# One VectorE sum of 1024 inputs in place of two of 512 for the later modulation vectors

## The chip, the core and the metric

The kernel runs on one core of one Trainium2 chip. The number that counts is the device time in microseconds (us) of one execution. The engines are TensorE (PE in the profile, its weight loads PEld), VectorE (DVE), ScalarE (ACT), GpSimd (POOL) and SyncE (SP). SP computes nothing; its queue issues nearly all DMA loads and stores here, strictly in the order in which they were written.

## The reference, cut to what matters

One layer of a diffusion backbone over 1024 latent tokens and 256 context tokens, all in float32, with a width of 1024:

```python
mod = einsum('bd,dn->bn', silu(c), w_ada) + b_ada       # 1024 inputs -> 6 * 1024
sh1, sc1, g1, sh2, sc2, g2 = split(mod, 6)
xn  = rmsnorm(h) * (1 + sc1) + sh1
mix = output projection of (differential attention over 1280 keys, gated 3-tap convolution)
h   = h + g1 * rmsnorm(mix)
xn  = rmsnorm(h) * (1 + sc2) + sh2
ff  = expert-choice mixture of 16 experts (router, gate, up, down)
h   = h + g2 * rmsnorm(ff)
```

The "later modulation vectors" are the last four of the six, `g1, sh2, sc2, g2`. They are needed only after attention.

## The kernel before, in words

The program has three stretches. The first (up to about 217 us in the profile) normalises the tokens, computes `sh1` and `sc1` on TensorE, and projects queries, keys and values. The second (217 to about 757 us) is attention, with the convolution and the output projection as filling work. The third holds the 16 experts.

**Attention.** 32 steps, one for each pair of a head (two score maps each) and a tile of 128 queries. The score maps `ps` (twice 128x1280) take 12 matmuls (L1090); VectorE finds the two row maxima `nm` (L1099), ScalarE takes the exponentials `e` (L1103), VectorE joins the two maps (L1117), TensorE transposes the result (`ptr`, L1130), ScalarE and VectorE split it into a high and a low part `ath`, `atl` (L1135, L1138), and on every second step 30 matmuls `po` multiply by the values. There is one buffer `ps` in PSUM: the scores of a step cannot start before both exponentials of the step before have read it. Scores run two steps ahead of the transposes. The code ahead of the loop (L1202 to L1212) makes the maps of the first two steps; these are "the first maps".

**Filling work.** Between these, `fill(n)` puts n matmuls of other work on TensorE, first those of the convolution's projection (`pf`, L675 to L679): 24 behind the first maps, 36 behind the second, then 36 in each step. Their weights come as blocks `wraw` (512 KB, L635), which ScalarE and VectorE split into `wh` and `wl`.

**The later modulation vectors.** `rows()` (L698 to L734) is a generator that computes them on VectorE. `w_ada` is laid out so that 128 outputs stand on the 128 partitions and the 1024 inputs along each; `silu(c)` lies in `silub`, repeated on all partitions. One instruction multiplies a tile `wa2` by `silub` and adds up along the row (L717, its sum read out by a second, short instruction). There are 4 vectors of 8 blocks, so 32 rows of 1024 inputs, 64 halves. A half is loaded (256 KB, L708) into one of three buffers; the next load into a buffer waits until the sum that read it is done. Four halves are asked for in each of the first steps (L1285), and two behind each of the first maps (L1210, L1211). When all 8 blocks of `g1` or `g2` are there, a small store writes the vector to DRAM element by element (`bS`, L732), so that it can be read back on all partitions.

**What sets the order.** SP's order, and TensorE's up to step 0, are the order of the program text. VectorE, ScalarE and, from step 0 on, TensorE are ordered by the framework's scheduler, from its own estimate of when operands are ready. In each engine's queue an instruction that waits holds up all behind it.

Of the kernel before, what the change touches and what calls it, by code (L numbers as in the profile page):

```python
# [10 lines left out]
F32 = mybir.dt.float32  # L11
# [4 lines left out]
OP = mybir.AluOpType  # L16
# [4 lines left out]
P = 128  # L21
D = 1024
# [5 lines left out]
KT = 8  # L28
# [124 lines left out]
def build(tc, nc, I, out, dbg=None):  # L153
    V, S, G, PE, SY = nc.vector, nc.scalar, nc.gpsimd, nc.tensor, nc.sync
# [3 lines left out]
    def f(ap):  # L158
        return ap.bitcast(F32)
# [11 lines left out]
    with es:  # L171
# [4 lines left out]
        sm = es.enter_context(tc.tile_pool(name="sm", bufs=4))  # L176
# [4 lines left out]
        def pool(stack, name, bufs=1, **kw):  # L181
            return stack.enter_context(tc.tile_pool(name=name, bufs=bufs, reuse_waits="tile", **kw))
# [329 lines left out]
        for i in range(10):  # L512
# [6 lines left out]
            for j in range(2):  # L519
                S.dma_start(out=vS[:, :, j, i, :].rearrange("h p e -> p h e"),  # L520
                            in_=f(hl[:, j, :]).rearrange("p (h e) -> p h e", h=H))
# [53 lines left out]
        rwp = pool(eR, "rwp", 3)  # L575
# [122 lines left out]
        def rows():  # L698
            sb = rwp.tile([P, D], F32, name="silub", bufs=1)
            SY.dma_start(out=sb, in_=bass.AP(tensor=sS.tensor, offset=sS.offset, ap=[[0, P], [1, D]]))  # L700
            src = deque((v, k, g) for v in (1, 2, 0, 3) for k in range(KT) for g in range(2))
            ws = deque()

            def load():
                if src:
                    v, k, g = src.popleft()
                    ws.append((v, k, g, rwp.tile([P, 512], F32, name="wa2")))
                    SY.dma_start(out=ws[-1][3], in_=I["wa2"][v, k, :, 512 * g:512 * g + 512])  # L708

            for _ in range(3):  # L710
                load()
            while ws:
                yield
                v, k, g, w = ws.popleft()
                if g:
                    part = sm.tile([P, 1], F32, name="part")
                V.scalar_tensor_tensor(w, w, 1.0, sb[:, 512 * g:512 * g + 512], op0=OP.mult, op1=OP.mult,  # L717
                                       accum_out=part if g else mv[:, v, k:k + 1])
                load()
                if g == 0:  # L720
                    continue
                V.tensor_add(mv[:, v, k:k + 1], mv[:, v, k:k + 1], part)
                if k == KT - 1:
                    V.tensor_add(mv[:, v, :], mv[:, v, :], late["bC"][:, v, :])
                    if v != 1:
                        V.scalar_tensor_tensor(mv[:, v, :], mv[:, v, :], 1.0 if v == 2 else 0.0,
                                               late["nC"][:, max(v - 1, 0), :], op0=OP.add, op1=OP.mult)
                    if v == 2:
                        lazy.append(fold)
                    elif v != 1:  # L730
                        def send(v=v):
                            SY.dma_start(out=bS[v // 3].rearrange("o (k p) -> p (o k)", p=P), in_=mv[:, v, :])  # L732

                        lazy.append(send)  # L734


        mv = cp.tile([P, 4, KT], F32, name="mv")
# [10 lines left out]
        def fold2():  # L748
            pw = bank([P, E], "pw")
            PE.matmul(pw, ones.to_broadcast([P, P]), cst2, start=True, stop=True)  # L750
            V.tensor_copy(out=cst2, in_=pw)

        rowgen = rows()
        woh, wol, worw = [None] * KT, [None] * KT, {}
        st = [dict() for _ in range(KT)]
# [328 lines left out]
        def scores(q, KK):  # L1084

            ps = psS.tile([P, 2, NK], F32, name="ps")
            for m in range(2):
                for (k0, n) in CH[m]:
                    for j in range(2):
                        PE.matmul(ps[:, m, k0:k0 + n], q[:, m, j, :], KK[:, m, k0:k0 + n], start=(j == 0),  # L1090
                                  stop=(j == 1))
            return ps, []

        def maxes(c):
            c[1].extend([ep.tile([P, NK], F32, name="e0", bufs=3), ep.tile([P, NK], F32, name="e1"),
                         sm.tile([P, 2], F32, name="l")])
            for m in range(2):
                c[1].append(sm.tile([P, 1], F32, name=f"nm{m}"))
                V.tensor_reduce(out=c[1][-1], in_=c[0][:, m, :], axis=AX.X, op=OP.max, negate=True)  # L1099

        def expo(c, m):
            e, l = c[1][m], c[1][2]
            S.activation(e, c[0][:, m, :], AF.Exp, bias=c[1][3 + m], accum_out=l[:, m:m + 1])  # L1103
# [98 lines left out]
        for i in range(2):  # L1202
            cs.append(scores(qq[i], KK[0]))
            maxes(cs[i])
            expo(cs[i], 0)
            expo(cs[i], 1)
            fill(F0)
            combine(cs[i], i)
            tick()
            next(rowgen)  # L1210
            next(rowgen)  # L1211
            fill(F1 * i)  # L1212
        steps = []

# [4 lines left out]
        for i, (h, qt) in enumerate(seq):  # L1219
# [62 lines left out]
                    hi(x2)  # L1282
                    lo(x2)
            if i < 16:
                for _ in range(4):  # L1285
                    next(rowgen, None)
            step()
            if odd:
# [207 lines left out]
        for e in range(E):  # L1496
            idx, g = cur[:2]
# [23 lines left out]
            for c in range(2):  # L1521
                w = chunk(e, 4 + c)
# [7 lines left out]
            if e + 1 < E:  # L1530
                y = x1.tile([P, D], F32, name="y")
                for dh in range(2):
                    S.activation(y[:, dh * 512:dh * 512 + 512], pys[dh], AF.Copy, scale=g[:, 0:1])
                G.indirect_dma_start(out=ffS[:, :], out_offset=bass.IndirectOffsetOnAxis(ap=idx[:, :1], axis=0),
                                     in_=y, in_offset=None, compute_op=OP.add)
# [37 lines left out]
        for i, grp in enumerate(TGR):  # L1573
            w = len(grp)
# [29 lines left out]
```

## Time and profile before

| | us |
|---|---|
| median of 3 runs | 1399.57 (1394.0 to 1402.64) |
| the profiled execution | 1401.37 |
| its span on the core | 1399.6 |
| TensorE busy in the span | 1259.0 (90%) |
| VectorE busy | 1104.3 (79%) |
| ScalarE busy | 805.7 (58%) |
| mean granted TensorE clock | 0.941 of full speed |

All rows are from one profiled execution. The span is the time from the first to the last instruction of the core; the 1.8 us on top of it lie outside the recorded instructions. Busy shares are averages over stretches with different limits, so the timelines, the waits and the windows of a stretch say more than the shares do.

### The profile page before, as it was taken

The numbers are of one execution on the slowest core, as the hardware profiler recorded it, in microseconds if no ns is written. First come the engines' busy times: TensorE is split into PE (matmuls) and PEld (weight loads), VectorE is DVE, ScalarE is ACT, GpSimd is POOL, SyncE is SP. The second block draws the span as 40 slices with busy tenths as digits, with TensorE's granted clock in tenths as the row PEclk, the third lists the DMA queues.
The fourth block names the chain that finished last, engine by engine and source line by source line (L and its number), as shares of the span: only waits on it lengthen the run. The fifth ranks groups of instructions, "written<-read, shape, count | busy, mean of one in ns | idle before, by whom it ended". The sixth has DMA issues, their size and how long they took to land.

```text
span 1399.6 us, 18794 instructions
## 1 busy us (share of the span) xinstructions
PE 1259.0 (90%) x6457; PEld 1028.7 (73%) x6457; DVE 1104.3 (79%) x2005; ACT 805.7 (58%) x1191; POOL 70.8 (5%) x56
## 2 busy tenths in 40 slices
PE   6999998999989699789762999999999999999990
PEld 3587886887878578677652888888888888877770
DVE  6963666988778667698686799999999998888885
ACT  6632112443434444453331888888888888888762
POOL 0000000000000000000001000000000001201012
PEclk8999999999999899999775999999999999999995
DMA  9359456554486963432287899999999999999736
GB/s 351 117 109 325 133 159 208 162 164 136 142 160 182 235 218 110 136 124 95 76 311 275 278 364 389 374 376 376 379 373 378 377 379 379 354 345 350 267 120 120
DMA packets 143376, 346.67 MB, mean 248 GB/s; under 512 B 17456, under 2 KB 59952, under 8 KB 142640
## 3 DMA queue, kind: packets, MB, share of 16 engines
q1 hardware_dynamic: 115520, 310.34, 63.4%
q0 software_dynamic: 5616, 20.45, 6.1%
q10 hardware_dynamic: 22144, 14.68, 3.7%
q8 instruction: 51, 0.84, 0.2%
q14 instruction: 45, 0.37, 0.1%
HBM read 296.65 MB, written 48.77 MB: 247 GB/s over the span
## 4 chain that ended last, share of the span: by engine, by line
PE 47%; DVE 8%; ACT 2%; issue 1%; DMA 1%; SPq 0%; POOL 0%; POOLq 0%; ACTq 0%; DVEq 0%
PE hg L167 4%; PE hg L168 4%; PE hg L166 4%; PE hu L166 4%; PE hu L167 4%; PE hu L168 4%; PE pyy L167 4%; PE pyy L168 4%; PE pyy L166 4%; PE ptt L1479 2%; PE pl L921 1%; DVE nm L1099 1%; PE ptt L1451 1%; PE pf L799 1%; PE ps L1090 1%
## 5 line engine op out<-in xcount | busy, mean ns | idle before, releaser
L163 DVE TENSOR_TENSOR wlo<-raw,whi 128x1024 fp32r<-128x1024 f32 x384 | 450.1, 1221 | 30.8 <-ACT whi L162 24.5
L162 ACT ACTIVATE whi<-raw 128x1024 fp32r<-128x1024 f32 x384 | 396.1, 1066 | 61.7 <-PE hu L168 24.9
L1103 ACT ACTIVATE e<-ps,nm 128x1280 f32<-128x1280 f32 x64 | 84.4, 1325 | 68.5 <-DVE nm L1099 61.3
L1099 DVE TENSOR_REDUCE nm<-ps 128x1 f32<-128x1280 f32 x64 | 92.8, 1485 | 16.0 <-PE ps L1090 15.9
L167 PE MATMUL pyy<-wlo,ach 128*128 128x512 f32 x256 | 101.3, 396 | 3.5 <-DVE wlo L163 3.1
L166 PE MATMUL hu<-whi,xsh 128*128 128x512 f32 x256 | 101.9, 398 | 0.0
L168 PE MATMUL hg<-whi,xsl 128*128 128x512 f32 x256 | 101.2, 395 | 0.8 <-DVE xsl L163 0.8
L167 PE MATMUL hg<-wlo,xsh 128*128 128x512 f32 x256 | 101.8, 398 | 0.0
L166 PE MATMUL hg<-whi,xsh 128*128 128x512 f32 x256 | 101.3, 396 | 0.0
L167 PE MATMUL hu<-wlo,xsh 128*128 128x512 f32 x256 | 100.8, 394 | 0.0
L168 PE MATMUL pyy<-whi,acl 128*128 128x512 f32 x256 | 100.2, 391 | 0.0
L168 PE MATMUL hu<-whi,xsl 128*128 128x512 f32 x256 | 99.9, 390 | 0.0
L1135 ACT ACTIVATE ath<-ptr 128x512 fp32r<-128x512 f32 (+1 forms) x96 | 47.5, 525 | 90.7 <-PE ptr L1130 90.4
L166 PE MATMUL pyy<-whi,ach 128*128 128x512 f32 x256 | 98.9, 402 | 0.0
L1090 PE MATMUL ps<-KK,q 128*128 128x512 f32 (+1 forms) x384 | 91.0, 384 | 7.8 <-ACT e L1103 6.2
L1090 PEld LDWEIGHTS ps<-KK,q 128*128 128x128 f32 x384 | 65.1, 202 | 18.8 <-ACT e L1103 7.4
L679 PE MATMUL pf<-xh,wl 128*128 128x512 f32 x192 | 77.7, 405 | 0.0
L677 PE MATMUL pf<-xl,wh 128*128 128x512 f32 x192 | 77.3, 403 | 0.0
L675 PE MATMUL pf<-xh,wh 128*128 128x512 f32 x192 | 77.0, 401 | 0.0
L1138 DVE TENSOR_TENSOR atl<-ptr,ath 128x512 fp32r<-128x512 f32 (+1 forms) x96 | 55.6, 596 | 13.8 <-ACT ath L1135 13.6
L167 PEld LDWEIGHTS pyy<-wlo,ach 128*128 128x128 f32 x256 | 48.2, 188 | 18.0 <-DVE wlo L163 8.2
L167 PEld LDWEIGHTS hg<-wlo,xsh 128*128 128x128 f32 x256 | 48.9, 191 | 11.5 <-DVE wlo L163 1.1
(293 smaller groups left out, 2728.8 us busy)
## 6 DMA issues: line engine op xcount, KB each, us to landing
raw<-in_we SPq DMA_DIRECT2D x384, 512.0 KB, 9.5
wa<-in_wa SPq DMA_DIRECT2D x64, 256.0 KB, 4.8
wraw<-in_wF SPq DMA_DIRECT2D x20, 512.0 KB, 6.4
waw<-in_wa SPq DMA_DIRECT2D x16, 512.0 KB, 5.9
q<-qS SPq DMA_DIRECT2D x64, 128.0 KB, 4.9
mS<-hl SPq DMA_DIRECT2D x48, 128.0 KB, 4.2
vS<-hv ACTq DMA_DIRECT2D x20, 256.0 KB, 6.5
KK<-kS SPq DMA_DIRECT2D x16, 320.0 KB, 4.9
```

What stands on the lines that cost most here:

```text
L162: S.activation(hi, src, AF.Copy)
L163: eng.tensor_sub(lo, src, f(hi))
L166: PE.matmul(ps, wh, mh, start=first, stop=False)
L167: PE.matmul(ps, wh, ml, start=False, stop=False)
L168: PE.matmul(ps, wl, mh, start=False, stop=last)
L675: PE.matmul(ps, wh[:, kt, :], xh[kt][:, sl], start=first, stop=False)
L677: PE.matmul(ps, wh[:, kt, :], xl[kt][:, sl], start=False, stop=False)
L679: PE.matmul(ps, wl[:, kt, :], xh[kt][:, sl], start=False, stop=last)
L1090: PE.matmul(ps[:, m, k0:k0 + n], q[:, m, j, :], KK[:, m, k0:k0 + n], start=(j == 0), stop=(j == 1))
L1099: V.tensor_reduce(out=c[1][-1], in_=c[0][:, m, :], axis=AX.X, op=OP.max, negate=True)
L1103: S.activation(e, c[0][:, m, :], AF.Exp, bias=c[1][3 + m], accum_out=l[:, m:m + 1])
L1138: V.tensor_sub(x[1], x[2], f(x[0]))
```

## The change

A row is loaded and summed whole: 32 loads of 512 KB into two buffers in place of 64 of 256 KB into three, 32 sums over 1024 inputs in place of 64 over 512, and no addition of two halves. Each of the first 16 steps asks for two rows; the calls behind the first two maps are gone. The bytes loaded are the same.

```diff
-            src = deque((v, k, g) for v in (1, 2, 0, 3) for k in range(KT) for g in range(2))
+            src = deque((v, k) for v in (1, 2, 0, 3) for k in range(KT))
...
-                    v, k, g = src.popleft()
-                    ws.append((v, k, g, rwp.tile([P, 512], F32, name="wa2")))
-                    SY.dma_start(out=ws[-1][3], in_=I["wa2"][v, k, :, 512 * g:512 * g + 512])
-
-            for _ in range(3):
+                    v, k = src.popleft()
+                    ws.append((v, k, rwp.tile([P, D], F32, name="wa2", bufs=2)))
+                    SY.dma_start(out=ws[-1][2], in_=I["wa2"][v, k])
+
+            for _ in range(2):
                 load()
             while ws:
                 yield
-                v, k, g, w = ws.popleft()
-                if g:
-                    part = sm.tile([P, 1], F32, name="part")
-                V.scalar_tensor_tensor(w, w, 1.0, sb[:, 512 * g:512 * g + 512], op0=OP.mult, op1=OP.mult,
-                                       accum_out=part if g else mv[:, v, k:k + 1])
+                v, k, w = ws.popleft()
+                V.scalar_tensor_tensor(w, w, 1.0, sb, op0=OP.mult, op1=OP.mult, accum_out=mv[:, v, k:k + 1])
                 load()
-                if g == 0:
-                    continue
-                V.tensor_add(mv[:, v, k:k + 1], mv[:, v, k:k + 1], part)
...
             combine(cs[i], i)
             tick()
-            next(rowgen)
-            next(rowgen)
             fill(F1 * i)
...
-                for _ in range(4):
+                for _ in range(2):
                     next(rowgen, None)
```

**VectorE at the first maps.** This is VectorE's queue from the last instruction of the projections on (`hl`), before:

```order
L454 SCALAR_TENSOR_TENSOR hl<-t_1745,hl 128x512
L717 SCALAR_TENSOR_TENSOR wa_1830,mv<-wa_1830,silub 128x512
L717 SCALAR_TENSOR_TENSOR wa_1832,part<-wa_1832,silub 128x512
L722 TENSOR_TENSOR mv<-mv,part 128x1
L717 SCALAR_TENSOR_TENSOR wa_1834,mv<-wa_1834,silub 128x512
L1099 TENSOR_REDUCE nm_1883<-ps 128x1
L1099 TENSOR_REDUCE nm_1885<-ps 128x1
L1116 SCALAR_TENSOR_TENSOR lq<-l 128x1
```

And the same place now:

```order
L454 SCALAR_TENSOR_TENSOR hl<-t_1745,hl 128x512
L715 SCALAR_TENSOR_TENSOR wa_1830,mv<-wa_1830,silub 128x1024
L1093 TENSOR_REDUCE nm_1881<-ps 128x1
L1093 TENSOR_REDUCE nm_1883<-ps 128x1
L715 SCALAR_TENSOR_TENSOR wa_1832,mv<-wa_1832,silub 128x1024
L1110 SCALAR_TENSOR_TENSOR lq<-l 128x1
L1107 RECIPROCAL r<-l 128x1
```

Ahead of the first maxima stood three sums of halves, from three loads; now the scheduler has put one sum of a whole row there, from one load, although the text asks for it only in step 0.

**SP at a block of convolution weights.** SP's queue in step 6, before (`mS` are stores of finished attention blocks, `hl` their source):

```order
L708 DMA wa_2948<-in_wa 128x512
L708 DMA wa_2952<-in_wa 128x512
L708 DMA wa_2956<-in_wa 128x512
L708 DMA wa_2960<-in_wa 128x512
L617 DMA mS<-hl_2878 128x2x128 x2
L635 DMA wraw<-in_wF 128x1024
```

And now:

```order
L1068 DMA q<-qS_74 64x2x256 x2
L708 DMA wa_2870<-in_wa 128x1024
L708 DMA wa_2873<-in_wa 128x1024
L617 DMA mS<-hl_2800 128x2x128 x2
L635 DMA wraw<-in_wF 128x1024
```

The weights stood behind four loads that wait for VectorE's sums, and stand behind two.

**SP at the small store of `g1`.** Before, at the end of step 10 and in step 11:

```order
L732 DMA bS<-mv 128x8x1
L617 DMA mS<-hl_3592 128x2x128 x2
L1074 DMA q<-qS_74 64x2x256 x2
L708 DMA wa_3676<-in_wa 128x512
L708 DMA wa_3680<-in_wa 128x512
```

And now, at the end of step 11 and in step 12:

```order
L726 DMA bS<-mv 128x8x1
L1068 DMA q<-qS_74 64x2x256 x2
L1062 DMA KK<-kS_79 64x1280 x4
L753 DMA woraw<-in_wO 128x1024 x3
L708 DMA wa_3702<-in_wa 128x1024
L708 DMA wa_3705<-in_wa 128x1024
```

The store moved one step back, past the step's loads. The next load of a row now also has the keys of a head (`KK`, 1.25 MB) and three blocks of the output projection's weights (`woraw`, 1.5 MB) between the store and itself. VectorE's queue where that load is used, now:

```order
L1132 TENSOR_TENSOR atl_3695<-ptr,ath_3694 128x2x128
L208 TENSOR_TENSOR nz_3711<-nz_3711 128x4
L1109 TENSOR_SCALAR s_3731<-r,l,neglam 128x1
L209 TENSOR_TENSOR nz_3711<-nz_3711 128x4
L715 SCALAR_TENSOR_TENSOR wa_3702,mv<-wa_3702,silub 128x1024
L212 SCALAR_TENSOR_TENSOR nz_3711<-nz_3711 128x4
L1111 SCALAR_TENSOR_TENSOR e_3655<-e_3656,s_3731,e_3655 128x1280
```

It stands at the end of step 12, ahead of the joining of the maps of step 14; before, the sum behind the store stood ahead of the third `atl` of step 11.

## Rows read from the trace of the kernel before

**Rows 1.** The page, part 1: busy time, share of the span, instructions

```profile
PE   1259.0 (90%) x6457; PEld 1028.7 (73%) x6457; DVE 1104.3 (79%) x2005; ACT 805.7 (58%) x1191; POOL 70.8 (5%) x56
```

**Rows 2.** Windows of two stretches; busy us of each engine, clock, DMA share, GB/s

```profile
420.00:470.00 50.00, 43.51 (x234) 36.93 (x232) 42.11 (x89) 21.33 (x38) 0.00 (x0) 0.89 0.74 223
...
800.00:1400.00 600.00, 562.60 (x2908) 460.18 (x2906) 524.57 (x580) 483.91 (x629) 63.55 (x39) 0.97 0.93 335
```

**Rows 3.** Timeline of VectorE at the first maps: start, us, what, idle before it

```profile
219.27 0.69 DVE L717 SCALAR_TENSOR_TENSOR wa<-wa,silub 128x512 f32<-128x512 f32 x1 [3.08 <-DMA wa<-in_wa]
...
224.23 0.69 DVE L717 SCALAR_TENSOR_TENSOR wa<-wa,silub 128x512 f32<-128x512 f32 x1 [3.31 <-DMA wa<-in_wa]
...
224.85 2.88 DVE L1099 TENSOR_REDUCE nm<-ps 128x1 f32<-128x1280 f32 x2
```

**Rows 4.** Timeline of TensorE there: last filling matmul, scores of the second maps

```profile
224.38 0.39 PE L679 MATMUL pf<-xh,wl 128*128 128x512 f32 x1
230.61 4.64 PE L1090 MATMUL ps<-KK,q 128*128 128x512 f32 x12 [5.84 <-ACT e L1103]
```

**Rows 5.** Timeline of SP there, and landing of the loads issued from 213 to 225

```profile
213.22 7.31 SPq L708 DMA_DIRECT2D wa<-in_wa  x3
...
DMA to landing us min/median/max: 4.0/5.2/6.3
```

**Rows 6.** Windows behind four waits of TensorE: length, PE busy, clock, DMA share, GB/s

```profile
230.00:236.00 6.00, 5.39 (x15) 0.50 0.42 134
...
338.00:342.00 4.00, 4.00 (x14) 0.64 0.30 109
...
415.00:421.00 6.00, 6.00 (x17) 0.50 0.83 225
...
498.00:501.00 3.00, 2.26 (x10) 0.76 0.44 130
```

**Rows 7.** Timeline of TensorE, the shortest of these four waits

```profile
498.74 0.44 PE L1130 MATMUL ptr<-ident,e 128*128 128x128 f32 x2 [2.23 <-DVE atl L1138]
```

**Rows 8.** Timelines of SP, ScalarE and TensorE around the late block of weights

```profile
323.29 4.81 SPq L708 DMA_DIRECT2D wa<-in_wa  x4
...
329.18 0.51 SPq L635 DMA_DIRECT2D wraw<-in_wF  x1
...
336.03 1.06 ACT L162 ACTIVATE wh<-wraw 128x1024 fp32r<-128x1024 f32 x1 [4.07 <-DMA wraw<-in_wF]
...
337.63 0.61 PE L1173 MATMUL px<-ones,sq 128*128 128x1 f32 x4 [3.00 <-ACT u L683]
```

**Rows 9.** Around the small store: SP, DMA window, landing of the next `wa`, VectorE, TensorE

```profile
398.71 0.56 SPq L732 DMA_DIRECT2D bS<-mv  x1
...
405.00:410.00 5.00, 5.00 (x36) 1.00 1.02 71
...
DMA to landing us min/median/max: 10.6/10.6/10.6
...
413.84 0.69 DVE L717 SCALAR_TENSOR_TENSOR wa<-wa,silub 128x512 f32<-128x512 f32 x1 [6.42 <-DMA wa<-in_wa]
...
414.94 0.58 PE L167 MATMUL po<-atl,vv 128*128 128x256 f32 x1 [4.72 <-DVE atl L1138]
```

**Rows 10.** Groups by line: busy, mean ns, idle before; sums, additions, a 1024-wide operation

```profile
L717 DVE SCALAR_TENSOR_TENSOR wa<-wa,silub 128x512 f32<-128x512 f32 x64 | 43.3, 686 | 14.4 <-DMA wa<-in_wa 14.2
...
L657 DVE SCALAR_TENSOR_TENSOR gc<-u,cw,gc 128x1024 f32<-128x1024 f32 x8 | 10.2, 1277 | 0.0
...
L722 DVE TENSOR_TENSOR mv<-mv,part 128x1 f32<-128x1 f32 x32 | 4.9, 152 | 0.1
```

**Rows 11.** The page, part 6: loads of 256 KB and 512 KB, median us to landing

```profile
wa<-in_wa SPq DMA_DIRECT2D x64, 256.0 KB, 4.8
wraw<-in_wF SPq DMA_DIRECT2D x20, 512.0 KB, 6.4
```

**Rows 12.** Timeline of TensorE where VectorE has no idle time

```profile
456.49 1.11 PE L1130 MATMUL ptr<-ident,e 128*128 128x128 f32 x4 [3.55 <-DVE atl L1138]
```

## The prediction

> **What bounds the kernel now.** I read the page's busy shares first, then the windows by stage, then the waits of TensorE in the stretch that the change touches, and last the timelines around each wait. TensorE is busy for 1259.0 us of the span [rows 1], and in the experts for 562.6 of 600 us [rows 2]. Nothing of the change runs there, and what those engines do depends on one another and not on the clock on the wall. So a microsecond won before 757 us is a microsecond at the end, as long as nothing later waits for something that did not also come earlier. In attention TensorE has holes, and VectorE is busy in 42.1 of 50 us in the fullest window [rows 2]. The reader is to see three of these holes, since each hangs on the sums or on their loads.
>
> First, the front. VectorE stands still for 3.08 us for the first load of `wa` and, two sums later, for 3.31 us for the third [rows 3]; only then come the maxima, which start at 224.85. The scores of the second maps start at 230.61, 5.76 us later, and TensorE has by then been idle for 5.84 us, since its 24 filling matmuls ran out [rows 4]. Second, the weights. A block `wraw` is issued at 329.18, behind four loads of `wa` that SP spends 4.81 us on; ScalarE waits 4.07 us for it, and TensorE 3.00 us for ScalarE [rows 8]. Third, the small store. `bS` goes out at 398.71; from 405 to 410 the DMA engines are full (share 1.02) and move 71 GB/s, against 335 in the experts [rows 2, 9]. The load behind it takes 10.6 us, VectorE waits 6.42 us for it, and TensorE 4.72 us for an `atl` queued behind that sum [rows 9].
>
> **A wait costs more than its length.** The granted clock was at its lower level (0.50, which is 1.2 GHz) for 5.39 busy us behind the first hole and for 6.00 behind the third: half of it is lost, 2.7 and 3.0 us. Behind the 3.00 us hole it was 0.64 for 4 us, which loses 1.4 [rows 6]. Behind one of 2.23 us [rows 7] it was 0.76 on average in a window of 3 us with 2.26 busy [rows 6], so even that short a hole may cost something like 1.4 in all, which I take for any hole of 2 to 3 us.
>
> **The change part by part**, against the profiled execution's own 1401.37 us.
>
> *The sums themselves.* A pair of halves takes 2 x 686 + 152 ns, a whole row should take the 1277 ns of the other operation of this kind that is 1024 wide [rows 10]: 0.25 us less, 32 times, 8 us of VectorE. I count none of it. Where VectorE has idle time it only grows that idle time. In the one stretch where VectorE has none and TensorE waits for it, the 3.55 us at 456.49 [rows 12], the order of work before that `atl` holds nearly as many sums as before. If that cover were gone there, it would be worth under 1 us. 32 fewer issues on SP and 32 fewer additions go with it, also at nothing.
>
> *The front.* The order now has one whole row ahead of the first maxima instead of three halves. Its load has no row. The nearest are the first loads there, issued from 213.2 on and landed after at most 6.3 us [rows 5]; both halves of the first row were there by about 220.0, and the bytes ahead of them on the queue are the same. So the whole row is there at 220.0, is summed by 221.3, and the maxima start then. With the 5.76 us of before, scores start at 227.1, after a hole of 2.3 instead of 5.84: 3.5 us. The lower clock costs 1.4 instead of 2.7: 1.3 us. Together **-4.8**. Bounds: if the load came as late as the third half did (224.2), the maxima would start at 225.5, +0.7; if it never held the maxima up, hole and clock go whole, -8.5. I take the one nearest to the first two loads.
>
> Behind the maxima stands the second row. Its load is issued with the first now, where the third half waited on SP until the last of the 7.31 us [rows 5], so I charge it nothing; what stands behind it (the joining of the first maps) is wanted only after 36 filling matmuls.
>
> *The weights.* SP reaches `wraw` behind two loads, whose buffers come free with sums that VectorE now does before the joining of the maps, where the last of the four was released after it. A few microseconds earlier would close the 4.07 us wait, and with it 3.00 + 1.4 = 4.4 us. Whether the page of memory that `wraw` goes into is free then I cannot read. Between 0 and -4.4 I take the middle, **-2.2**.
>
> *The small store.* The load after it is no longer needed in the step after; the third `atl` of step 11 has no sum in front of it whose load is behind the store. 4.72 + 3.0 = 7.7 us go. What is late next: `wa_3702`, behind the store, the keys and the three weight blocks. The store seems to hold the queue for some 11 us, then about 3.5 MB at between 225 and 335 GB/s take 10 to 15; the load would be there 24 to 29 us after the transposes of step 11, and its sum stands 25 to 26 us after them. Bounds for what comes back: 0 and the same 7.7. I take 2.5, since most of that interval lies before the sum: **-5.2**.
>
> Other steps: each load of 512 KB needs some 6.4 us where a half needed 4.8 [rows 11], is issued when the row two before is summed, and is wanted a step later. With steps of 12 us or more I charge nothing; what it would cost is a rival below.
>
> Sum: -4.8 - 2.2 - 5.2 = -12.2, so 1389.2 for an execution like the profiled one. The median of the runs shown is 1.8 below that execution, hence 1387.4; I say **1388**.
>
> **The rivals.**
>
> *All three holes close and nothing takes their place.* For it: TensorE's filling work is the same in number, and its order hardly moves. Against it: the scheduler reorders much on VectorE. -4.8 - 4.4 - 7.7 = -16.9, so 1383. Chance 0.25.
>
> *The front closes wholly.* If the first load is there before the first scores end, the front gives -8.5 and the sum is -15.9, 1384. The trace speaks against it, as half as many bytes took up to 6.3 us at that place [rows 5], with the stores of the projections on the same DMA engines. Chance 0.07. By the Trainium skill (page "DMA: Bandwidth & Descriptors", section "Anatomy of one DMA — SWDGE (gpsimd) path") a load costs about 2.0 us plus its bytes at 436 GB/s, an estimate of 3.2 us for 512 KB, and this would be the case. [...]
>
> *The store's hole only moves.* The load behind `bS` is as late for its new place as it was for the old one, and `wraw` is held by its page. Then the front alone is left: 1399.6 - 4.8 = 1395. For it: more bytes than ever stand between the store and that load. Chance 0.25.
>
> *Slower: two buffers are too few.* A load can go out only when the row two before is summed, and the two sums of a step often stand together. If a load takes over 10 us, as behind the store [rows 9], in more than two steps, the sum waits, and with it the maxima or `atl` queued behind. Each such wait costs what the third hole costs, 7.7 us. Three of them beside the front's gain: +23 - 5, so 1418. Against it: outside the store a block of 512 KB lands in 6.4 us. Chance 0.08.
>
> **How the numbers follow.** The forecast has 0.33, and 0.02 is for none of these. About 1%, 14 us, is what a measurement of this kernel can tell from no change. Under 1385.6 lie most of the first two rivals (0.25) and the better third of the forecast (0.11): 0.36. Over 1413.6 lies the last rival: 0.08. The rest is 0.56. The range leaves out the slower rival and the tails: from 1376, the first rival with the front closed wholly and some luck, to 1401, the third rival with the front at its worse bound.
>
> **What would show it.** Maxima of the first maps starting near 221.3, and a hole of TensorE near 2.3 us before the second scores; ScalarE's wait for the `wraw` of step 6 under 1 us; no hole of several microseconds in `po` of step 11; VectorE's wait at the sum behind `bS` under 2 us. The prediction is wrong if VectorE's total wait for `wa` stays near the 14.2 us of before [rows 10], or if new holes of over 2 us with the lower clock behind them stand where there was none.

## The result: 17 us faster

The changed kernel takes 1382.5 us in the median of 5 runs (1378.3 to 1386.9), the kernel before 1399.6. The ratio is 0.987, with a 95% interval of 0.983 to 0.991. The profiled execution of the changed kernel took 1378.3 (span 1376.5, against 1399.6), the quickest of its five, so the two traces differ by 23.1 us where the medians differ by 17. So some 6 of the 23.1 us belong to the two executions that happened to be profiled, and not to the change.

Where the 23.1 us come from is read from TensorE's 32 groups of 12 score matmuls, the same work in the same order in every kernel here. The table gives when the n-th group starts in the kernel before, and how much earlier (minus) or later it starts in the others. The first group, ahead of which no edit does anything to TensorE's work, already starts up to 1.3 us earlier and 0.9 later than in the kernel before, and behind the 22nd group kernels move by up to 4 us against each other without a cause in these traces. So single microseconds are not to be read.

| kernel | 3rd | 9th | 10th | 14th | 15th | 18th | 19th | 22nd | 32nd | span |
|---|---|---|---|---|---|---|---|---|---|---|
| before, us | 244.8 | 328.6 | 345.6 | 401.2 | 424.3 | 460.0 | 487.7 | 520.2 | 661.1 | 1399.6 |
| **the change** | -4.0 | -4.6 | -9.2 | -8.0 | -15.8 | -16.7 | -25.0 | -19.0 | -20.4 | -23.1 |
| e1 | -1.6 | +0.9 | +1.3 | +2.8 | -5.0 | +5.1 | +4.0 | +11.7 | +12.4 | +11.1 |
| e2 | -2.4 | -3.7 | -8.3 | -8.2 | -7.2 | -8.2 | -7.3 | -10.5 | -10.6 | -11.1 |
| e3 | -2.2 | -2.4 | -0.7 | -0.7 | -8.5 | +0.7 | +1.9 | +0.3 | +3.9 | +3.3 |
| e4 | -2.7 | -3.1 | -7.7 | -6.3 | -3.1 | -1.2 | -2.1 | -3.7 | 0.0 | -2.4 |
| a4 | -1.7 | -1.7 | -1.5 | -1.5 | -9.3 | -9.0 | -15.3 | -15.3 | -11.7 | -14.9 |
| a1 | -5.1 | -5.9 | -10.4 | -9.1 | -16.9 | -13.7 | -22.2 | -22.6 | -22.6 | -22.6 |
| a2 | -8.7 | -9.1 | -13.6 | -12.3 | -20.1 | -21.0 | -29.1 | -23.6 | -25.6 | -26.4 |
| a3 | -5.7 | -6.0 | -10.6 | -9.3 | -17.1 | -16.4 | -23.1 | -23.7 | -25.1 | -25.9 |
| a5 | -4.9 | -5.2 | -9.8 | -9.6 | -8.7 | -9.6 | -12.5 | -15.7 | -15.9 | -16.0 |
| a6 | -4.1 | -5.4 | -9.8 | -8.7 | -16.5 | -7.8 | -15.2 | -9.1 | -10.5 | -13.6 |
| a7 | -4.2 | -5.0 | -9.6 | -8.1 | -15.8 | -16.8 | -25.0 | -25.4 | -25.3 | -25.4 |
| a8 | -8.0 | -8.4 | -13.0 | -11.5 | -19.3 | -20.2 | -28.7 | -29.1 | -29.1 | -29.8 |

In the row of the change there are four steps down and one step up: the front (4.0 by the third group), the weights (4.6 between the 9th and the 10th), the small store (7.8 between the 14th and the 15th), one that was not forecast (8.3 between the 18th and the 19th), and then 6.0 given back by the 22nd. Another 4.1 by the end of the span have no cause that I can show; a1 and a7 have nothing of the kind, and the medians differ by less. The front's 4.0 is too much as well: five kernels below leave the front alone (e1 to e4 and a4), and their third group comes 1.6 to 2.7 us earlier than in the kernel before too. Measured from the first group to the third, the six kernels with the old front take 25.9 to 28.0 us (mean 26.9) and the five with the new one (the change, a1, a5, a6, a7) 23.0 to 24.4 (mean 23.7), so the front is worth about 3.

**The front.** Timelines of VectorE and TensorE of the changed kernel at the first maps, and the window behind the hole (length, PE busy and then the other engines, clock, DMA share, GB/s). They answer to [rows 3, 4, 6].

```profile
220.93 1.23 DVE L715 SCALAR_TENSOR_TENSOR wa<-wa,silub 128x1024 f32<-128x1024 f32 x1 [4.38 <-DMA wa<-in_wa]
...
222.08 2.88 DVE L1093 TENSOR_REDUCE nm<-ps 128x1 f32<-128x1280 f32 x2
```
```profile
227.83 3.91 PE L1084 MATMUL ps<-KK,q 128*128 128x512 f32 x12 [2.73 <-ACT e L1097]
```
```profile
227.00:233.00 6.00, 5.17 (x18) 4.26 (x19) 3.95 (x5) 2.33 (x4) 0.00 (x0) 0.72 1.04 349
```

One sum of a whole row still stands ahead of the maxima, which now start at 222.08 and not at 224.85. The hole is 2.73 us where it was 5.84 (5.04 to 6.00 in the other kernels with the old front, 2.09 to 3.48 in those with the new one). Why the third half was so late in the kernel before is seen in SP's waits (line, what it waited for: us in total, times, longest), before and after:

```profile
SPq L708 <- DMA qS<-hl: 6.0, 1, 6.0
```
```profile
SPq L1073 <- DMA qS<-hl: 7.6, 1, 7.6
```

In the kernel before, SP stood for 6.0 us of [rows 5] at one of the three loads, until a store of the projections (`qS`) had landed. With two loads that wait falls on the load after them, `vv`, which no sum needs.

**The weights.** Timelines of SP, ScalarE and TensorE of the changed kernel; they answer to [rows 8].

```profile
316.30 2.35 SPq L708 DMA_DIRECT2D wa<-in_wa  x2
...
320.67 0.35 SPq L635 DMA_DIRECT2D wraw<-in_wF  x1
```
```profile
326.54 1.06 ACT L162 ACTIVATE wh<-wraw 128x1024 fp32r<-128x1024 f32 x1 [1.15 <-DMA wraw<-in_wF]
```
```profile
330.02 0.61 PE L1167 MATMUL px<-ones,sq 128*128 128x1 f32 x4
```

The block of weights is issued at 320.67, behind the two loads of its step, where it was behind four of them at 329.18. SP stood 1.0 us for its page of memory, which a `pf` matmul still read. ScalarE waits 1.15 us for it instead of 4.07, and TensorE not at all.

**The stores.** `bS` is stored twice. The first store falls at 395.61 now; VectorE's waits for `wa` over the whole kernel, which were 14.2 us [rows 10], are down to these (us, times, longest), and neither is behind the store:

```profile
DVE wa L715 <- DMA wa<-in_wa: 5.1, 2, 4.4
```

The step at the 19th group is at the second store, which the prediction did not look at. In the kernel before, the last block of the output projection's weights goes out 0.78 us ahead of it. Timelines of SP, ScalarE and TensorE of the kernel before, with the landing of that `woraw`:

```profile
469.13 0.47 SPq L759 DMA_DIRECT2D woraw<-in_wO  x1
469.91 0.36 SPq L732 DMA_DIRECT2D bS<-mv  x1
```
```profile
DMA to landing us min/median/max: 10.7/10.7/10.7
```
```profile
479.87 1.06 ACT L162 ACTIVATE woh<-woraw 128x1024 fp32r<-128x1024 f32 x1 [4.84 <-DMA woraw<-in_wO]
```
```profile
481.46 0.50 PE L799 MATMUL pf<-woh,mA 128*128 128x512 f32 x1 [3.79 <-ACT res L810]
```

In the changed kernel the block goes out at 454.10 and the store only at 459.41. That block lands in 4.8 us, in time; what is late instead is a query behind the store. SP, the two queries' landing, TensorE and the window at the hole, of the changed kernel:

```profile
459.41 1.01 SPq L726 DMA_DIRECT2D bS<-mv  x1
...
464.92 2.34 SPq L1068 DMA_DIRECT2D q<-qS  x2
```
```profile
DMA to landing us min/median/max: 13.8/14.5/15.2
```
```profile
480.60 4.44 PE L1084 MATMUL ps<-KK,q 128*128 128x512 f32 x12 [4.28 <-DMA q<-qS]
```
```profile
478.00:482.00 4.00, 1.40 (x3) 1.16 (x4) 0.00 (x0) 0.00 (x0) 0.00 (x0) 0.50 0.15 52
```

The two loads of 128 KB take 13.8 and 15.2 us, TensorE waits 4.28 us, and the clock is at its lower level (0.50) afterwards. That is what is given back after the 19th group.

### The profile page after: what moved, and what is told of

It is laid out like the page before. It is cut to its first block, busy times and chain, and to the rows that moved or that the text cites. A ratio compares the mean times of both kernels' runs of the same rounds, so it can differ in the third digit from the quotient of the medians.

```text
span 1376.5 us, 18654 instructions
## 1 busy us (share of the span) xinstructions
PE 1249.9 (91%) x6457; PEld 1021.0 (74%) x6457; DVE 1099.6 (80%) x1909; ACT 805.4 (59%) x1191; POOL 68.2 (5%) x56
## 4 chain that ended last, share of the span: by engine, by line
PE 47%; DVE 8%; ACT 2%; issue 2%; DMA 1%; POOL 0%; POOLq 0%; ACTq 0%; DVEq 0%
PE hg L167 4%; PE hg L168 4%; PE hg L166 4%; PE hu L166 4%; PE hu L167 4%; PE hu L168 4%; PE pyy L167 4%; PE pyy L168 4%; PE pyy L166 4%; PE ptt L1471 2%; PE pl L915 1%; DVE nm L1093 1%; PE ptt L1443 1%; PE pf L793 1%; PE pf L797 1%
## 5 line engine op out<-in xcount | busy, mean ns | idle before, releaser
L163 DVE TENSOR_TENSOR wlo<-raw,whi 128x1024 fp32r<-128x1024 f32 x384 | 450.2, 1219 | 29.4 <-ACT whi L162 24.4
L1093 DVE TENSOR_REDUCE nm<-ps 128x1 f32<-128x1280 f32 x64 | 92.6, 1483 | 19.3 <-PE ps L1084 19.2
L1132 DVE TENSOR_TENSOR atl<-ptr,ath 128x512 fp32r<-128x512 f32 (+1 forms) x96 | 55.5, 594 | 13.7 <-ACT ath L1129 13.2
```

What stands on the lines that cost most here:

```text
L163: eng.tensor_sub(lo, src, f(hi))
L1132: V.tensor_sub(x[1], x[2], f(x[0]))
```

## The experiments

The theory: the gain is TensorE's holes that close, each for a reason of its own on a queue (a third load that waits, a block of weights behind loads, a store of single elements with something wanted behind it), and VectorE's saved time is worth nothing. The rivals: the missing calls, the depth of the buffers, or the shorter sums are what pays. All times are medians, with the ratio to the kernel before on the same chip (its medians there are 1399.1 to 1400.6).

| kernel | us | ratio, 95% interval |
|---|---|---|
| e1: before, two calls removed | 1412.5 | 1.008 (1.006 to 1.011) |
| e2: before, four buffers | 1388.5 | 0.990 (0.987 to 0.994) |
| e3: before, first store a step later | 1400.9 | 1.000 (0.998 to 1.002) |
| e4: before, step 6 reordered | 1398.3 | 0.998 (0.996 to 1.000) |
| a4: before, stores in runs of 32 bytes | 1384.9 | 0.990 (0.988 to 0.992) |
| a1: changed, second store at the end | 1374.8 | 0.982 (0.979 to 0.986) |
| a2: changed, no sum in front | 1376.7 | 0.985 (0.983 to 0.987) |
| a3: a1 and a2 | 1372.1 | 0.981 (0.979 to 0.984) |
| a5: changed, two calls back | 1384.6 | 0.988 (0.985 to 0.991) |
| a6: changed, each sum in halves | 1390.0 | 0.993 (0.990 to 0.996) |
| a7: changed, stores in runs of 32 bytes | 1372.8 | 0.980 (0.978 to 0.983) |
| a8: a7 and a2 | 1371.2 | 0.980 (0.977 to 0.983) |

### The parts of the change, one at a time

**e1**, the calls alone, on the kernel before:

```
             tick()
-            next(rowgen)
-            next(rowgen)
             fill(F1 * i)
```

> The kernel before without the two calls behind each of the first maps; the sums stay 512 wide. Theory of the three holes: only the front can close. VectorE then has one half sum instead of three ahead of the first maxima, its second wait there (3.31 us) goes, and the hole of TensorE before the second scores shrinks by 3 to 5 us; the weights' hole and the store's hole move but do not go, since their order on SP is the same. The time falls by 3 to 5 us, to 1395 to 1397. Rival (what pays is VectorE's own work, 8 us less of it): no sum is removed here, so the time is that of before, within 1.5 us.

Measured 11.9 us slower, which neither side expected. The front hardly moved: three halves still stand ahead of the maxima, where one was expected (the order places sums of the first steps there), the third waits 2.21 us, and TensorE's hole is 5.83. Everything else came later by one or two steps of sums, and met other things. SP, its waits and TensorE of e1:

```profile
415.08 0.42 SPq L732 DMA_DIRECT2D bS<-mv  x1
...
461.86 12.12 SPq L708 DMA_DIRECT2D wa<-in_wa  x4
```
```profile
SPq L708 <- DVE wa L717: 8.8, 2, 8.6
```
```profile
440.94 0.80 PE L675 MATMUL pf<-xh,wh 128*128 128x512 f32 x1 [7.05 <-DVE gc L693]
...
483.27 0.77 PE L799 MATMUL pf<-woh,mA 128*128 128x512 f32 x1 [9.34 <-DMA mA<-mS]
...
511.40 4.60 PE L1090 MATMUL ps<-KK,q 128*128 128x512 f32 x12 [5.27 <-DMA q<-qS]
```

The first store's hole only moved (7.05 us). At 461.86 SP stood for 12.12 us at four loads, 8.6 of it until a sum freed a buffer, and the loads of the output projection queued behind cost TensorE 9.34. The second store has its hole too (5.27). So the removed calls are no gain in themselves on that kernel.

**e2**, deeper buffers alone (as many bytes as the changed kernel keeps):

```
-ws.append((v, k, g, rwp.tile([P, 512], F32, name="wa2")))
+ws.append((v, k, g, rwp.tile([P, 512], F32, name="wa2", bufs=4)))
...
-            for _ in range(3):
+            for _ in range(4):
```

> The kernel before with four buffers of 512 for the loads in place of three, which are the bytes that the changed kernel keeps. Theory of the three holes: a load more ahead does not change what stands in front of the first maxima (three half sums) nor that the store goes out element by element, but the load behind the store is wanted one sum later. Gain 0 to 5 us, most of it at the store, and the front's hole of 5.84 us stays. Rival (depth of the buffers is what pays, not where the sums stand): the whole gain of the change, about 17 us, so 1383.

1388.5 is 12 us less, between the two and nearer to the rival. The place was not the one expected. The table shows 4.6 us between the 9th and the 10th group, the weights' hole, closed as in the changed kernel; the third half still waits 2.21 us in front. So depth alone does part of the change's work, by what it lets SP issue earlier. The first store kept its hole (5.61 us of TensorE). About 3 us more come from the 19th to the 22nd group: that stretch takes 32.4 us in the kernel before, with the hole of 2.23 us of [rows 7] in it and a mean granted clock of 0.95, and 29.3 us in e2, where TensorE waits 0.24 us and the clock is 1.00. So that hole cost some 2 us of idle time and 1 of clock; why its `atl` is no longer late in e2 I did not trace.

**e4**, the order on SP in one step alone:

```
-            if i < 16:
+            if i < 16 and i != 6:
                 for _ in range(4):
                     next(rowgen, None)
...
             tick()
+            if i == 6:
+                for _ in range(4):
+                    next(rowgen)
```

> The kernel before with the four calls of step 6 alone moved behind that step's output projection, so that the weight block issued there stands ahead of four loads on SP instead of behind them. Theory: ScalarE's wait of 4.07 us for that block falls under 1 us, and TensorE's hole of 3.00 us with the clock behind it goes: 3 to 4.6 us, 1395 to 1396.5. Rival (the page of memory of the block is not free earlier, and the order on SP does not matter): ScalarE waits as long, and the time is that of before within 1.5 us.

Between the 9th and 10th group 4.6 us went, at the upper end of what was expected, and ScalarE no longer waited for the block. This shows that the weights' hole was the order on SP. But the median is only 2.3 us less, with no change inside the interval, and above the range expected, since the first store fell elsewhere and cost more. SP, VectorE and TensorE of e4:

```profile
393.56 0.45 SPq L732 DMA_DIRECT2D bS<-mv  x1
...
398.52 16.51 SPq L708 DMA_DIRECT2D wa<-in_wa  x4
```
```profile
413.97 0.69 DVE L717 SCALAR_TENSOR_TENSOR wa<-wa,silub 128x512 f32<-128x512 f32 x1 [10.90 <-DMA wa<-in_wa]
```
```profile
420.35 1.11 PE L1130 MATMUL ptr<-ident,e 128*128 128x128 f32 x4 [10.33 <-DVE u L685]
```

### The stores

**e3**, the first store held back one step:

```
-                        lazy.append(send)
+                        (held if v == 0 else lazy).append(send)
...
+            if i == 11:
+                lazy.extend(held)
```

> The kernel before with the store of the second gate vector (the element by element one at 398.71) held back until the step after; nothing else. Theory: the load that was late behind it (10.6 us) is then ahead of it, VectorE's wait of 6.42 us and TensorE's of 4.72 us behind it go with the low clock after them, 7.7 us; what is behind the store then is late next, 0 to 5 us come back. 1392 to 1397. Rival (the hole is the third query's transposes, whatever VectorE waits for): no change, 1398 to 1401.

No change, which is the rival's number but not for its reason. The table tells why: 7.8 us were won by the 15th group and 9.2 lost by the 18th. The hole had moved one step on, to the next load behind the store (VectorE and TensorE of e3):

```profile
435.22 0.69 DVE L717 SCALAR_TENSOR_TENSOR wa<-wa,silub 128x512 f32<-128x512 f32 x1 [5.83 <-DMA wa<-in_wa]
```
```profile
436.66 0.79 PE L675 MATMUL pf<-xh,wh 128*128 128x512 f32 x1 [6.18 <-DVE gc L693]
```

**a4**, the kernel before with stores in longer runs:

```
-SY.dma_start(out=bS[v // 3].rearrange("o (k p) -> p (o k)", p=P), in_=mv[:, v, :])
+SY.dma_start(out=bS[v // 3].rearrange("o (p k) -> p (o k)", p=P), in_=mv[:, v, :])
```

> The kernel before with both stores of a gate vector written in runs of eight elements for each partition, in place of single elements; the order of the elements in these two vectors is left out (it is permuted, and so are the gates). Theory: the cost is that of 1024 single writes of 4 bytes; with 128 writes of 32 bytes the load behind it lands in 5 to 6 us instead of 10.6, VectorE's wait of 6.42 us falls under 2 us and TensorE's hole of 4.72 us goes: 5 to 8 us less than before, and the wait for the last output weights at 470 to 488 may shrink too (up to 8 us more). Rival (bytes queued ahead are what makes that load late): the wait stays, and the time is that of before within 1.5 us.

1384.9, 14.2 us less, with none of the change in it (the two gate vectors come out in another order here, and nothing puts them back). The first step is 7.8 us between the 14th and 15th group, as expected, and 6.3 come between the 18th and the 19th, the second store's place. VectorE waits 0.29 us where it waited 6.42. Landing of the second store in a4, and of the last `woraw` ahead of it:

```profile
DMA to landing us min/median/max: 3.3/3.3/3.3
```
```profile
DMA to landing us min/median/max: 3.6/3.6/3.6
```

The 512 KB land in 3.6 us where they took 10.7, with the same 4 KB stored 0.5 us behind them. DMA packets of the kernel before, and of a4:

```profile
DMA packets 143376, 346.67 MB, mean 248 GB/s; under 512 B 17456, under 2 KB 59952, under 8 KB 142640
```
```profile
DMA packets 141584, 346.67 MB, mean 250 GB/s; under 512 B 15664, under 2 KB 58160, under 8 KB 140848
```

That is 1792 packets less, which is twice 1024 - 128: the store goes out as one packet for each element of 4 bytes. By the Trainium skill (page "DMA: Bandwidth & Descriptors", section "Rules for kernel authors") a strided last dimension becomes one descriptor per element and is to be rearranged; the count here agrees.

**a1**, the changed kernel with the second store behind the last attention step:

```
-                        lazy.append(send)
+                        (held if v == 3 else lazy).append(send)
...
+        lazy.extend(held)
         while steps:
```

> The changed kernel with the store of the last gate vector (the second element by element store, issued at 459.41) held back behind the last attention step, where no load of attention stands behind it. Theory: the new hole of TensorE of 4.28 us at 480.60, which waits for a query that landed 13.8 to 15.2 us after its issue behind this store, goes with the low clock after it: 5 to 7 us less than the changed kernel, 1376. Rival (the query is late for the mass of weights in front of it, not for the store): the hole stays and the time is that of the changed kernel within 1.5 us; or the held store meets the loads of the experts and 0 to 4 us come back there.

The query's hole is gone, and the table shows it: from the 18th to the 22nd group the changed kernel gains 2.3 us on the kernel before, a1 8.9. In its profile 3.2 us had been lost ahead of that, at the first store, where a load is now a little late (VectorE waits 3.02 us for it, and TensorE stands still for 2.35 us at the `pf` behind). It is 3.6 us ahead of the changed kernel at the 22nd group, 2.2 at the 32nd and 0.5 behind at the end of the span, which is that of the changed kernel's quickest run; I cannot say what takes these back. The median is 7.7 us under that of the changed kernel; the intervals of the two ratios overlap, so that the time alone does not settle it.

**a7**, the changed kernel with both stores in runs of 32 bytes, by the order in which weights, bias and norm vector are laid out ahead of the launch:

```
+    def pk(m, vs):
+        for v in vs:
+            m[v] = m[v].reshape(P, KT, *m.shape[3:]).swapaxes(0, 1)
+        return m
...
-SY.dma_start(out=bS[v // 3].rearrange("o (k p) -> p (o k)", p=P), in_=mv[:, v, :])
+SY.dma_start(out=bS[v // 3].rearrange("o (p k) -> p (o k)", p=P), in_=mv[:, v, :])
```

> The changed kernel with both gate vectors kept in an order in which a partition holds eight neighbouring elements (the weights, the bias and the norm vector are laid out so ahead of the launch), so that each store is 128 runs of 32 bytes in place of 1024 single elements. Theory: no transfer behind a store is late any more; the hole of 4.28 us at the query behind the second store goes with the low clock after it, 5 to 7 us less than the changed kernel, 1375 to 1378; the first store's place costs nothing now and gives nothing. Rival (the mass of bytes queued there makes the query late): within 1.5 us of the changed kernel.

1372.8, some 10 us under the changed kernel, which is more than was expected. Up to the 19th group it runs level with it, as expected; there the two part by 6.4 us. At the end of the spans 2.3 of that are left, but the profile is of the slowest of a7's runs and of the quickest of the changed kernel's. The same two queries, issued at 464.77, now land so:

```profile
DMA to landing us min/median/max: 7.1/7.3/7.5
```

So half of the 14.5 us of a query behind the store was the store's doing, and that half is the hole: TensorE does not wait for this query in a7. The other 7.3 us are there without single elements too. From a4 to a7, both without stores of single elements, the rest of the change is worth 12 us in the median; in the table it is 2.5 us at the third group and 8.1 at the 10th, behind the weights.

### The front, the calls and the sums

**a2**, the changed kernel with the start of `rows()`, which issues `silub` and the first two loads, moved behind the first maps, so that no sum can stand ahead of them:

```
         qq = [load_q(*seq[i]) for i in range(3)]
-        next(rowgen)
...
             fill(F1 * i)
+        next(rowgen)
```

> The changed kernel with its one sum ahead of the first maps moved behind them. Theory: VectorE's last wait there (4.38 us for the first load) is no longer in front of the maxima, TensorE's hole of 2.73 us before the second scores goes with the clock behind it: 3 to 5 us less, about 1378. Rival (the hole is held by what follows the maxima, the exponentials and the joining, not by the sum): under 1.5 us.

The maxima start at 218.17, as soon as the scores are there, and TensorE's hole is gone (TensorE of a2):

```profile
223.93 2.59 PE L1084 MATMUL ps<-KK,q 128*128 128x512 f32 x12 [0.34 <-ACT e L1097]
```

In the profile the third group is 4.7 us earlier than in the changed kernel, though 1.5 of that is there at the first group already, and 3.3 are left at the end. The median is 5.8 less, with overlapping intervals. The query's hole is still there, 3.25 us. The edit moves the loads on SP as well as the sum on VectorE, behind `vv` and a block of weights, so the gain cannot be put down to the sum's place alone.

**a3** and **a8** are a2 together with a1 and with a7.

> Both together: the changed kernel with its last store behind the last attention step, and with no sum ahead of the first maps. Theory: the two gains lie in different places and add: 8 to 12 us less than the changed kernel, 1371 to 1375. Rival (a gain in front only moves work into the next wait): no more than the larger of the two alone.

> The same stores in runs of 32 bytes, and no sum ahead of the first maps. Theory: the two gains lie in different places and add, 8 to 11 us less than the changed kernel, 1371 to 1375. Rival (holding the store back is as good): the same 1372 as the version that holds the second store back and has no sum in front.

Both are within what was expected, 1372.1 and 1371.2. But by the times alone a3 cannot be told from a1, nor a8 from a7 or a3, so neither rival is excluded by them. The interval of a8 lies wholly under that of the changed kernel, and its profile shows the two gains added: 4.0 us at the third group over the changed kernel, and 6.1 more by the 22nd. In a3's profile the front closed only in part, to 2.02 us: ScalarE waited 4.69 us there for a block of weights ahead of its exponentials.

**a5**, the changed kernel with a call behind each first map put back:

```
             tick()
+            next(rowgen)
             fill(F1 * i)
```

> The changed kernel with one call for a sum behind each of the first two maps put back, so that the sums run two rows further ahead. The same edit the other way round on the kernel before cost it 12 us, since SP stood 12.12 us at loads of sums in front of the last weights. Theory (with two whole-row buffers SP no longer stands long at these loads, so what counts is only where the stores fall): the last load goes out a step earlier, both stores go out a step earlier, and the time moves by 5 us at most either way. Rival (the number of sums ahead of the steps is what the change's gain rests on): back up by 8 us or more, to 1390 or over.

1384.6, the time of the changed kernel within the intervals. In the profile the front is the same (a hole of 2.89 us), but the first store goes out 10 us earlier, at 385.79, and TensorE has the hole of the kernel before again, 6.07 us at 407.16; the query's hole is gone in exchange. In the changed kernel, then, the number of calls shows only in where the stores fall.

**a6**, the changed kernel with each sum in two halves:

```
...
+                for g in range(2):
+                    c = slice(512 * g, 512 * g + 512)
+                    V.scalar_tensor_tensor(w[:, c], w[:, c], 1.0, sb[:, c], op0=OP.mult, op1=OP.mult,
+                                           accum_out=part if g else mv[:, v, k:k + 1])
+                V.tensor_add(mv[:, v, k:k + 1], mv[:, v, k:k + 1], part)
```

> The changed kernel with its loads, buffers and calls, but each sum made of two halves and an addition again, as before; VectorE has about 8 us more to do. Theory (VectorE's saved time is worth nothing, loads and their order are): the time of the changed kernel within 2 us, 1380 to 1385. Rival (the shorter sums are the gain, or part of it): 4 to 8 us more, 1387 to 1391.

1390.0, which is the rival's number, 7.5 us over the changed kernel (all its runs lie above all of the changed kernel's; the intervals of the two ratios just overlap). Its place is not the rival's, though. By the 15th group 24 of the 32 rows are summed, and a6 is no later than the changed kernel (-16.5 against -15.8): the longer sums cost nothing there. All the loss is in one hole. SP, the landing of the load at 415.53, VectorE and TensorE of a6:

```profile
400.89 0.36 SPq L731 DMA_DIRECT2D bS<-mv  x1
...
408.59 6.24 SPq L758 DMA_DIRECT2D woraw<-in_wO  x3
415.53 1.68 SPq L708 DMA_DIRECT2D wa<-in_wa  x2
```
```profile
DMA to landing us min/median/max: 11.7/11.7/11.7
```
```profile
427.23 0.69 DVE L718 SCALAR_TENSOR_TENSOR wa<-wa,silub 128x512 f32<-128x512 f32 x1 [8.92 <-DMA wa<-in_wa]
```
```profile
430.19 0.79 PE L675 MATMUL pf<-xh,wh 128*128 128x512 f32 x1 [7.75 <-DVE gc L693]
```

The first store goes out 5.3 us later than in the changed kernel, and the loads behind it 8.8 us later; SP itself waits 2.3 us for the store to land before it issues a `woraw`. The store is late because SP waits 4.3 us for the finished vector `mv`, and that is a matter of VectorE's order. The last steps of `mv` (adding `bC`, multiplying by `nC`) and the maxima `nm` of that place, in the changed kernel and in a6:

```profile
391.52 0.16 DVE L718 TENSOR_TENSOR mv<-mv,bC 128x8 f32<-128x8 f32 x1
...
395.43 0.15 DVE L720 SCALAR_TENSOR_TENSOR mv<-mv,nC 128x8 f32<-128x8 f32 x1
...
396.64 2.88 DVE L1093 TENSOR_REDUCE nm<-ps 128x1 f32<-128x1280 f32 x2
```
```profile
396.88 2.88 DVE L1098 TENSOR_REDUCE nm<-ps 128x1 f32<-128x1280 f32 x2
399.68 0.16 DVE L723 TENSOR_TENSOR mv<-mv,bC 128x8 f32<-128x8 f32 x1
...
400.70 0.16 DVE L725 SCALAR_TENSOR_TENSOR mv<-mv,nC 128x8 f32<-128x8 f32 x1
```

In a6 the scheduler put both behind the maxima and not ahead of them. The last row was complete, its two halves added, at 394.7, and the changed kernel's store went out only at 395.61. So the sums were done in time in a6 as well, and what came late was the rest of `mv`. The edit changes two things, the length of the sums and the order that the scheduler makes of them, and the trace puts the loss on the order. In the changed kernel the same loads went out at 406.75, and the first of them was summed at 418.93 without a wait. Their landing is not on record; if it took the 9.9 us of the slowest load of a row in that trace, the margin was some 2 us (an estimate). A version of a6 with short-run stores, or with its `mv` ahead of the maxima, would show whether the longer sums cost anything by themselves; neither was run.

## Why the prediction came out right, and where its terms did not

The time was forecast as 1388 and is 1382.5, within the range; the mechanism, holes of TensorE that close, is what the experiments show. The three holes close much as in the first rival, whose sum of -16.9 is also the number measured; but that nothing takes their place is not so. Two terms that no one forecast, -8.3 and +6.0, largely cancel, and that is luck. The terms:

- *The front*, -4.8: measured -4.0 by the third group, and about -3 against all kernels with the old front. The maxima start at 222.08 and not at 221.3, since the sum of the first row began 7.35 us after the issue at 213.58, where the loads of [rows 5] landed in at most 6.3, and the hole is 2.73 and not 2.3. That load is also why the front did not close wholly. The section of the Trainium skill that the prediction names at the rival in which it does close is on DMAs issued by GpSimd, and these loads are issued by SP. Right in mechanism, and too large in size. That the number of calls does not set what stands in front is shown by e1 and a5; the expectation of e1 had that wrong.
- *The weights*, -2.2 out of 0 to -4.4: measured -4.6. The page of memory came free 1.0 us after SP had reached the block, and the whole hole closed. e4 gives the same 4.6 by the order on SP alone, so the term was only mis-sized.
- *The small store*, -5.2, of which 2.5 was to come back: measured -7.8 at that place, with nothing back in this stretch. But the term had only one of the two stores in it. The second, at 469.91, held up a block of weights that had been issued ahead of it; its going from there came with another 8.3 (a4, by longer runs alone, gets 6.3 there), and its new place costs 6.0. The prediction's view, the load *behind* a store, missed what is in flight *before* it.
- *The sums themselves*, 0: right as far as VectorE's time goes. A whole row takes 1218 ns and not 1277, and the one stretch where VectorE has no idle time keeps its hole: 3.55 us before, 3.67 in the changed kernel, 3.94 in a6. The prediction had no term for what the form of the sums does to the scheduler's order and so to the store; a6 loses 7.5 us there.
- *The store's hole only moves*, the rival with 0.25, is close to what e1, e2, e3, e4, a5 and a6 show: a hole stays behind their first store or moves with it, of 5.6 to 10.3 us. The changed kernel escaped it by a margin that I estimate at 2 us, so this term too came out by some luck. The prediction weighed it as one chance in four, from bytes in the queue; what counts in these traces is how long after the store the next wanted load is issued and how soon its sum is wanted.
- *Slower: two buffers are too few* did not happen: VectorE's waits for `wa` are 5.1 us in two places, one of them the front.

Of the marks set beforehand, the maxima (222.08 against 221.3), the weights (1.15 against under 1) and the total of waits (5.1 against 14.2) came near, and `po` of step 11 has no hole. A new hole of over 2 us with the low clock did come, at the query; it was named as what would make the prediction wrong, and it was outweighed by the gain at the block of weights.

## What to carry to other kernels

A small store with a strided destination belongs in the sum by its single elements, not by its bytes (whether their number or their size makes it slow is not separated here): look at what is in flight around it on the same queue, ahead as well as behind, and lay the data out for longer runs before moving it to another place. Where such a store stands in a tuned order, an edit that shifts it by 5 us can win or lose a whole hole, so compare the same milestones of work in both traces before crediting the edit with the difference. An edit to work off the critical path can still cost by the order that a scheduler makes of it: look at what sets the moment at which the next transfer goes out.

## What the runs showed of the hardware

4 KB stored in 1024 pieces took 9.2 to 17.7 us to land in these kernels, and in 128 pieces 1.4 to 7.0. Three pairs at the same place show what such a store does to its neighbours. A block of 512 KB issued ahead of it landed in 10.7 us (the kernel before), and in 3.6 with longer runs (a4). The keys issued behind the first store, 320 KB each, landed in 11.9 to 12.5 us in the changed kernel and in 5.3 to 6.7 in a7. The two queries behind the second store, 128 KB each, landed in 13.8 and 15.2 us, and in 7.1 and 7.5 in a7. SP itself stands longer too: with single elements the profile ends one of its waits, the longest 5.1 us (a1), at the landing of `bS` in every kernel here, and in a4, a7 and a8 none.
